# Stick-breaking attention summed by parts, with one sigmoid and the scan read from SBUF, in a hybrid SSM and attention block

## The chip, the cores and the metric

The kernel runs on one core of one Trainium2 chip. The core has five engines with queues of their own: TensorE (PE in the profile, with its weight loads apart as PEld), VectorE (DVE), ScalarE (ACT), GpSimd (POOL) and SyncE (SP), which here only issues DMAs. Instructions of one queue start in order; between queues they wait for semaphores. The metric is the device time of one execution in microseconds, as the median of several runs. Before the change it is 1559.6 us (three runs, 1559.3 to 1562.25).

## The reference, cut to what matters

One layer over 2048 tokens of width 1024. The input is normalised and projected; one half of the channels goes through a diagonal state-space model (SSM), the other half through stick-breaking attention with 8 heads of 64. Both are gated, projected out, added to the residual, and a gated embedding is added. The change touches the attention alone, and in it what follows the scores:

```python
z = jnp.einsum('bhqd,bhkd->bhqk', qb, kb) * scale
strict = s_pos < t_pos
log_stay = jnp.where(strict, jax.nn.log_sigmoid(-z), 0.0)
later = lax.cumsum(log_stay, axis=3, reverse=True) - log_stay
weights = jnp.where(strict, jnp.exp(jax.nn.log_sigmoid(z) + later), 0.0)
outs.append(jnp.einsum('bhqk,bhkd->bhqd', weights, vb))
```

For a query t and a key s before it, the weight is sigmoid(z[t, s]) times the product of sigmoid(−z[t, r]) over all r with s < r < t. Call P[s] the product over all r from s up to t − 1. Then the weight is P[s+1] − P[s], because 1 − sigmoid(−z) is sigmoid(z).

## The kernel before, in words

**Stages.** The SSM inputs are projected first, then comes the SSM with the gate's projections, then the attention, and at last the output projection and the embedding. The attention runs in 40 steps (`for t in range(steps)`). Four passes of two heads each (`hp`) start 8 steps apart, so that up to two passes are active in a step. In step t a pass computes the attention of query block i = t − 8 hp (`attn_block`, 128 queries), and then the projections of block i + 2 (`attn_proj`). In the last eight steps (from `glu_at` on) the SSM's output stage (`glu_unit`) and sums of weight blocks (`cross_sums`) are mixed in.

**Projections (`attn_proj`).** The normalised tokens `xt` come by a DMA on SP. PE multiplies them by one weight tile for q, k, v and the gate, in two halves of the contraction side by side, each into a PSUM bank of its own (`pq`, line 732). ACT copies the first bank to `part` (739, or 735 with a scale for the first two blocks), DVE adds the second: 384 columns to `qn` (740), 128 columns straight to the tile of v (741) that the attention multiplies later. The normalisation of q and k needs one power on POOL (501).

**Attention (`attn_block`).** Keys are taken in chunks of up to 512, from the newest back. Per chunk and for both heads:

1. PE writes the scores into a PSUM bank per head, `ps_z` (797). Up to step 31 three banks take turns (z0, z1, tr), in the last eight steps two (z0, z1).
2. ACT writes sigmoid(−z) to the SBUF tile `px` (802) and, after a border column was set by POOL (memset, 804) or copied by DVE from the chunk before (806), sigmoid(z) to the tile `be` (807).
3. In the newest chunk POOL masks the diagonal block of both tiles (811).
4. DVE turns `px` into running products from the right, in place (813). The scan is given the score bank as its second input; its second operation is a bypass, so that the values are not used.
5. POOL multiplies `be` by `px` shifted by one column (815). These are the weights.
6. PE transposes them into a pair of PSUM banks (`pw`, "ps_wt", line 520 of a helper), ACT copies them to `ws` (828), and PE multiplies them with v into `ps_o` (836). The same pair of banks also serves the transposes of q and k.

DVE multiplies the block's output by the gate into `yat`, and a DMA on SP stores it (840).

**Order.** All instructions get their place from a planner (`arrange`, `best_order`): it gives each an estimated duration, follows the dependences, keeps rows marked `abreast` together, and fixes the order on each queue, SP's DMAs among them. DVE operations with two SBUF inputs and POOL operations that read SBUF are planned one after the other. The buffers are counted by constants: `PXB` 4 tiles of `px`, `BEB` 6 of `be`. `BANKS` holds the PSUM banks of scores, projections and output, up to step 31 and after.

Of the kernel before, what the change touches and what calls it, by code (L numbers as in the profile page):

```python
# [18 lines left out]
P = 128  # L19
# [15 lines left out]
HD = 64  # L35
# [2 lines left out]
SKEW = 8  # L38
EPS = 1e-6
MAGIC = 12582912.0  # L40
XB, XTB, GTB, QSB, BEB, PXB, WSB, SWB, ROTB, STA, STB, STC, ALT, ALT0, ALT1, SSM_STEPS, SSM_DEPTH, PREP0, BEX, PXX, WSX, XTX, XT0 = 4, 2, 5, 5, 6, 4, 5, 2, 2, 3, 2, 3, "o", 0, 30, 10, 2, 0, 0, 0, 0, 0, 13
WE = 6
AHEAD = 4
BANKS = (("z0", "z1", "tr"), ("acc","ssm"), ("o",)), (("z0", "z1"), ("acc","tr"), ("o",))
WSV = lambda ch: 0
KV_SLOT = {(0, 0): 0, (0, 1): 1, (0, 2): 2, (1, 0): 3, (0, 3): 4, (1, 1): 5, (1, 2): 6, (2, 0): 7,
           (1, 3): 0, (2, 1): 1, (2, 2): 2, (3, 0): 4, (3, 1): 3, (2, 3): 5, (3, 2): 0, (3, 3): 1}
# [658 lines left out]
def attn_proj(e, pool, A, i, xt=None):  # L706

    nc = e.nc
    if xt is None:
        xt = e.buf("xt", [P, 2, NC8, P], XTB, XTX, F32R)  # L710
        e.xdma(xt.rearrange("p s c t -> p (s c t)").bitcast(F32), e.hn_d[i])
    both = pool.tile([P, 3 * HPP, HD], F32, tag="qn", name="qn", bufs=2)
    vb = A.v[i] = e.kv_tile(A.hp, i, "v", [P, HPP, HD])
    flat, vf = both.rearrange("p h d -> p (h d)"), vb.rearrange("p h d -> p (h d)")
    if len(e.q_banks) == 1:
        pq = e.bank("ps_qk", *e.q_banks)
        for c in range(NC8):
            mm3x(e, pq, (xt[:, 0, c], xt[:, 1, c]), (A.w[c][:, 0], A.w[c][:, 1]), c == 0, c == NC8 - 1)
        if i < 2:
            nc.scalar.activation(flat, pq[:, :384], AF.Copy, scale=e.rs[i])  # L720
            vs(nc, vf, pq[:, 384:], e.rs[i], ALU.mult)
        else:
            nc.scalar.activation(flat, pq[:, :384], AF.Copy)
            nc.vector.tensor_copy(vf, pq[:, 384:])
    else:
        pq = [e.bank(f"ps_q{h}", tag) for h, tag in enumerate(e.q_banks)]
        for c in range(NC8):
            with e.abreast():
                for s, (a, b) in enumerate(((0, 0), (0, 1), (1, 0))):
                    for h, o in enumerate(pq):  # L730
                        r = slice(64 * h, 64 * h + 64)
                        nc.tensor.matmul(o, xt[r, a, c], A.w[c][r, b], start=c + s == 0, stop=c == NC8 - 1 and s == 2)  # L732
        part = pool.tile([P, 512], F32, tag="part", name="part", bufs=1)
        if i < 2:
            nc.scalar.activation(part, pq[0], AF.Copy, scale=e.rs[i])
            stt(nc, flat, pq[1][:, :384], e.rs[i], part[:, :384], ALU.mult, ALU.add)
            stt(nc, vf, pq[1][:, 384:], e.rs[i], part[:, 384:], ALU.mult, ALU.add)
        else:
            nc.scalar.activation(part, pq[0], AF.Copy)
            vt(nc, flat, pq[1][:, :384], part[:, :384], ALU.add)  # L740
            vt(nc, vf, pq[1][:, 384:], part[:, 384:], ALU.add)
    raw, gate = both[:, :2 * HPP], flat[:, 256:]
    gn = pool.tile([P, P], F32, tag="gn", name="gn", bufs=1)
    nc.scalar.activation(gn, gate, AF.Sigmoid)
    vt(nc, gn, gate, gn, ALU.mult)
    sq = pool.tile([P, 2 * HPP, HD], F32, tag="sq", name="sq", bufs=1)
    nc.scalar.activation(sq, raw, AF.Square)
    ss = pool.tile([P, 2 * HPP], F32, tag="ssq", name="ssq", bufs=2)
    nc.vector.tensor_reduce(ss, sq, op=ALU.add, axis=AX.X)
    r = rms_rstd(e, pool, ss, 2 * HPP, HD, "qk")  # L750
    vt(nc, raw, raw, r.unsqueeze(2).to_broadcast([P, 2 * HPP, HD]), ALU.mult)
    qn = raw.rearrange("p (m h) d -> p m h d", m=2)
    if i % 4 == 0:
        A.k.append(e.kv_tile(A.hp, i, "k", [P, 2, 512]))
    q = pool.tile([P, 2, P], F32R, tag="q", name="q", bufs=QSB)
    views = [qn[:, m].rearrange("p h d -> p (h d)") for m in range(2)] + [gn]

    def whole(a):
        return a.rearrange("p (h t) -> p h t", h=2)

    if len(e.q_banks) == 1:
        ps = e.bank("ps_tq", "w0", "w1")
        for m, v in enumerate(views):
            nc.tensor.transpose(ps[:, m * P:(m + 1) * P], v, e.ident)
        tq, tk, tg = (whole(ps[:, P * m:P * m + P]) for m in range(3))
    else:
        ps = e.pair("ps_tq")
        with e.abreast():
            transposes(e, [ps[:, h] for h in range(2)], views)
        tq, tk, tg = (ps[:, :, 64 * m:64 * m + 64] for m in range(3))  # L770
    split(e, whole(q[:, 0]), whole(q[:, 1]), tq)
    k = A.k[-1][:, :, (i % 4) * P:(i % 4 + 1) * P]
    nc.scalar.activation(whole(k[:, 0]), tk, AF.Copy, scale=e.gqk)
    stt(nc, whole(k[:, 1]), tk, e.gqk, whole(k[:, 0]).bitcast(F32), ALU.mult, ALU.subtract)
    g = pool.tile([P, P], F32, tag="g", name="g", bufs=QSB)
    nc.scalar.activation(whole(g), tg, AF.Copy)
    A.q[i] = q, g


def attn_block(e, pool, A, i):  # L780

    nc = e.nc
    q, g = A.q.pop(i)
    half = [slice(HD * h, HD * (h + 1)) for h in range(HPP)]
    carry = [None] * HPP
    po = e.bank("ps_o", *e.o_banks)
    held = []
    for ch in range(i // 4, -1, -1):  # L790
        nb = min(4, i + 1 - 4 * ch)
        n = nb * P
        zs = [e.bank("ps_z", *e.z_banks) for _ in range(HPP)]
        with e.abreast():
            for s, (a, b) in enumerate(((0, 0), (0, 1), (1, 0))):
                for h, z in enumerate(zs):
                    nc.tensor.matmul(z[:, :n], q[half[h], a], A.k[ch][half[h], b, :n], start=s == 0, stop=s == 2)  # L797
        bes = []
        for h, z in enumerate(zs):
            be = e.buf("be", [P, 512], BEB, BEX)  # L800
            px = e.buf("px", [P, 513], PXB, PXX)
            nc.scalar.activation(px[:, :n], z[:, :n], AF.Sigmoid, scale=-(HD ** -0.5))  # L802
            if carry[h] is None:
                nc.gpsimd.memset(px[:, n:n + 1], 1.0)
            else:
                nc.vector.tensor_copy(px[:, n:n + 1], carry[h])
            nc.scalar.activation(be[:, :n], z[:, :n], AF.Sigmoid, scale=HD ** -0.5)  # L807
            if ch == i // 4:
                for a, fill in ((px, 1.0), (be, 0.0)):
                    d = a[:, n - P:n]  # L810
                    nc.gpsimd.affine_select(d, d, pattern=[[-1, P]], compare_op=ALU.is_gt, fill=fill, base=0, channel_multiplier=1)  # L811
            rv = px[:, :n][:, ::-1]
            nc.vector.tensor_tensor_scan(rv, rv, z[:, :n][:, ::-1], initial=1.0 if carry[h] is None else carry[h], op0=ALU.mult, op1=ALU.bypass)  # L813
            carry[h] = px[:, 0:1]
            nc.gpsimd.tensor_tensor(be[:, :n], be[:, :n], px[:, 1:n + 1], op=ALU.mult)  # L815
            bes.append(be)
        w = e.buf("ws", [P, HPP, 4, P], WSB, WSX)
        pw = e.pair("ps_wt")
        with e.abreast():
            transposes(e, [pw[:, h] for h in range(2)], [be[:, b * P:(b + 1) * P] for be in bes for b in range(nb)])  # L820
        for h in range(2):
            ps = pw[:, h, :64 * HPP * nb].rearrange("p (k t) -> p k t", t=64)
            dst = w[:, :, :nb, 64 * h:64 * h + 64]
            ps = ps.rearrange("p (h b) t -> p h b t", h=HPP)
            if h and WSV(ch):
                nc.vector.tensor_copy(dst, ps)
            else:
                nc.scalar.activation(dst, ps, AF.Copy)  # L828
        held.append((ch, nb, w))
        if len(held) == HOLD or ch == 0:  # L830
            with e.abreast():
                for c, n, w in held:
                    for b in range(n - 1, -1, -1):
                        sb = 4 * c + b
                        for h in range(HPP):
                            nc.tensor.matmul(po[half[h], :P], A.v[sb][:, h], w[:, h, b], start=sb == i, stop=sb == 0)  # L836
            held = []
    y = pool.tile([P, P], F32, tag="yat", name="yat", bufs=2)
    vt(nc, y, po[:, :P], g, ALU.mult)
    nc.sync.dma_start(e.ya_d[i][A.hp], y)  # L840


def attn_pass(e, hp):
    A = Env()
    A.hp, A.k, A.v, A.q, A.w = hp, [], {}, {}, []
    return A


# [178 lines left out]
def hybrid_block_kernel(ctx: ExitStack, tc: tile.TileContext, x, xt, small, p, w_in, ssm_w_glu, w_out, w_ple_gate,  # L1027
# [34 lines left out]
    make_identity(nc, e.ident)  # L1062
    e.mhalf = const("mhalf", [P, 2 * HPP])
    nc.vector.memset(e.mhalf, -0.5)
    e.rs = [const(f"rs{i}", [P, 1]) for i in range(2)]

    def part(name):
# [517 lines left out]
```

## Time and profile before

| | before |
|---|---|
| median of three runs | 1559.6 us |
| profiled execution | 1561.9 us |
| its span | 1560.2 us |
| PE, PEld busy | 1480.4, 1257.4 us |
| DVE, ACT, POOL busy | 1073.6, 938.7, 819.2 us |
| attention stage, 326.8 to 1166.8 us: span, PE busy | 840.0, 799.2 us |

How to read the rows: a group's row has line, engine, operation, output<-inputs, shapes and count; then busy us and the mean in ns of one; then the idle time of that engine just before, and what ended it. A row of a window has its length, then the busy time of each engine with its count, and at the end the clock that PE was granted (1.00 is full), the busy share of the DMA engines and GB/s. A row "A <- B: us, times, longest" is time in which A stood idle until B was done. "issue" is time in which an engine waited for nothing that the profile shows.

### The profile page before, as it was taken

To read this page: it belongs to the slowest core of one execution; us is meant where nothing else is said; L and a number is where in the kernel's file an instruction comes from. 1 tells how busy PE (TensorE), PEld (TensorE's weight loads), DVE (VectorE), ACT (ScalarE), POOL (GpSimd) and SP (SyncE) were. 2 spreads that over 40 slices of the span, in tenths; PEclk is the share of its full clock that TensorE was granted. 3 is DMA by queue.
4 is the path that set the end of the run, shared out by engine and by line. 5 is a ranking of instruction groups with operands and counts; after the bars stand their busy time and mean duration, and the time that the engine had idled before them with its cause. 6 is when DMAs were issued, how large, how long until landed. Compare 5 with 4: busy or idle time off the path is not lost.

```text
span 1560.2 us, 34921 instructions
## 1 busy us (share of the span) xinstructions
PE 1480.4 (95%) x13116; PEld 1257.4 (81%) x13116; DVE 1073.6 (69%) x2052; ACT 938.7 (60%) x2076; POOL 819.2 (53%) x1038
## 2 busy tenths in 40 slices
PE   5999999999999999998999988999998999999998
PEld 5999999978888788887887876777776888777776
DVE  8944868867667876778867776666869556754444
ACT  5654445557577877677777777766765435633432
POOL 3241433445455665565656688765565654433433
PEclk8999999999999989999999988999999999999999
DMA  8777735565332412234323466763448645612211
GB/s 294 272 250 222 237 119 188 165 198 163 116 116 99 150 67 98 105 116 128 99 94 112 138 213 180 220 184 93 112 136 257 199 161 183 200 63 94 89 62 61
DMA packets 168969, 236.21 MB, mean 151 GB/s; under 512 B 63664, under 2 KB 110816, under 8 KB 157408
## 3 DMA queue, kind: packets, MB, share of 16 engines
q1 hardware_dynamic: 166416, 225.38, 44.7%
q0 software_dynamic: 2384, 8.59, 2.0%
q8 instruction: 104, 1.70, 0.4%
q14 instruction: 65, 0.53, 0.1%
HBM read 169.03 MB, written 64.90 MB: 150 GB/s over the span
## 4 chain that ended last, share of the span: by engine, by line
PE 74%; DVE 9%; ACT 5%; issue 4%; DMA 4%; POOL 3%; POOLq 0%; SPq 0%; ACTq 0%; DVEq 0%
PE ps_q L732 19%; PE ps_o L836 6%; PE ps_z L797 5%; PE ps_wt L520 4%; PE ps_g L701 3%; PE ps_g L703 3%; PE ps_g L702 3%; PE ps_h L702 3%; PE ps_h L703 3%; PE ps_h L701 3%; DVE px L813 2%; PE ps_sg L535 2%; PE ps_sg L536 2%; PE ps_sg L537 2%; DMA wst<-in_ssm_w_glu_dram 2%
## 5 line engine op out<-in xcount | busy, mean ns | idle before, releaser
L815 POOL TENSOR_TENSOR be<-be,px 128x512 f32<-128x512 f32 (+3 forms) x320 | 317.6, 998 | 224.3 <-DVE px L813 177.1
L813 DVE TENSOR_TENSOR_SCAN px<-px,ps_z 128x512 f32<-128x512 f32 (+3 forms) x320 | 340.2, 1086 | 108.6 <-ACT be L807 81.8
L732 PE MATMUL ps_q<-w_w,xt 64*128 64x512 f32 x2880 | 400.9, 404 | 6.6 <-DVE v L65 3.6
L732 PEld LDWEIGHTS ps_q<-w_w,xt 64*128 64x128 f32 x2880 | 294.5, 187 | 43.8 <-PE ps_z L797 7.2
L828 ACT ACTIVATE ws<-ps_wt 128x512 f32<-128x512 f32 (+3 forms) x320 | 165.0, 547 | 76.2 <-PE ps_wt L520 75.9
L802 ACT ACTIVATE px<-ps_z 128x512 f32<-128x512 f32 (+3 forms) x320 | 162.4, 538 | 67.6 <-PE ps_z L797 48.7
L807 ACT ACTIVATE be<-ps_z 128x512 f32<-128x512 f32 (+3 forms) x320 | 168.7, 554 | 1.3 <-PE ps_wt L520 1.2
L797 PE MATMUL ps_z<-k,q 64*128 64x512 f32 (+3 forms) x960 | 146.3, 385 | 15.9 <-DVE px L813 12.4
L836 PE MATMUL ps_o<-ws,v 128*64 128x128 f32 x2176 | 139.8, 281 | 0.9 <-ACT ws L828 0.9
L836 PEld LDWEIGHTS ps_o<-ws,v 128*64 128x64 f32 x2176 | 121.0, 140 | 19.1 <-issue 15.5
L520 PEld LDWEIGHTS ps_wt<-ident,be 64*128 64x128 f32 x2176 | 101.1, 142 | 36.6 <-issue 15.3
L797 PEld LDWEIGHTS ps_z<-k,q 64*128 64x128 f32 x960 | 94.9, 189 | 35.0 <-DVE px L813 18.2
L520 PE MATMUL ps_wt<-ident,be 64*128 64x64 f32 x2176 | 108.5, 229 | 13.4 <-POOL be L815 4.8
L1008 POOL TENSOR_TENSOR sg<-sg,h 128x512 f32<-128x512 f32 x32 | 44.9, 1414 | 114.6 <-DVE sg L65 114.6
L501 POOL TENSOR_TENSOR rs_qk<-rs_qk,mhalf 128x4 f32<-128x4 f32 x64 | 66.6, 1040 | 39.7 <-DVE rs_qk L72 38.8
L535 PE MATMUL ps_u<-xt,w_w 128*128 128x256 f32 x256 | 74.8, 294 | 8.1 <-ACT w_w L485 7.0
L65 DVE TENSOR_TENSOR yr<-sx,yr 128x512 fp32r<-128x512 f32 x64 | 53.6, 858 | 34.6 <-ACT yr L507 33.7
L537 PE MATMUL ps_u<-xt,w_w 128*128 128x256 f32 x256 | 74.3, 296 | 3.0 <-DVE w_w L76 3.0
L536 PE MATMUL ps_u<-xt,w_w 128*128 128x256 f32 x256 | 74.8, 293 | 0.7 <-DVE xt L65 0.7
L507 ACT ACTIVATE yr<-sx 128x512 fp32r<-128x512 f32 x64 | 39.3, 629 | 50.8 <-POOL sx L894 20.2
L811 POOL TENSOR_SCALAR_AFFINE_SELECT px<-px 128x128 f32<-128x128 f32 x128 | 41.2, 332 | 50.4 <-ACT px L802 49.1
L1002 ACT ACTIVATE sg<-sg,rs 128x512 f32<-128x512 f32 x24 | 17.4, 724 | 73.6 <-DVE sg L65 73.6
(418 smaller groups left out, 3674.5 us busy)
## 6 DMA issues: line engine op xcount, KB each, us to landing
xt<-hn SPq DMA_DIRECT2D x60, 1024.0 KB, 4.9
hn<-xt SPq DMA_DIRECT2D x16, 1024.0 KB, 5.5
h<-h SPq DMA_DIRECT2D x64, 256.0 KB, 3.6
wst<-in_w_in_dram SPq DMA_DIRECT2D x48, 256.0 KB, 3.3
xg<-hn SPq DMA_DIRECT2D x12, 1024.0 KB, 6.7
out_dram<-sg SPq DMA_DIRECT2D x32, 256.0 KB, 2.5
x<-in_x_dram SPq DMA_DIRECT2D x14, 512.0 KB, 5.3
h<-in_x_dram SPq DMA_DIRECT2D x28, 256.0 KB, 4.7
```

The lines of the kernel that those rows point to most:

```text
L520: e.nc.tensor.transpose(ps[h][:, 64 * k:64 * k + 64], v[r], e.ident[r, r])
L535: mm(out, wh, xh, start=first, stop=False)
L536: mm(out, wh, xl, start=False, stop=False)
L537: mm(out, wl, xh, start=False, stop=last)
L732: nc.tensor.matmul(o, xt[r, a, c], A.w[c][r, b], start=c + s == 0, stop=c == NC8 - 1 and s == 2)
L797: nc.tensor.matmul(z[:, :n], q[half[h], a], A.k[ch][half[h], b, :n], start=s == 0, stop=s == 2)
L802: nc.scalar.activation(px[:, :n], z[:, :n], AF.Sigmoid, scale=-(HD ** -0.5))
L807: nc.scalar.activation(be[:, :n], z[:, :n], AF.Sigmoid, scale=HD ** -0.5)
L813: nc.vector.tensor_tensor_scan(rv, rv, z[:, :n][:, ::-1], initial=1.0 if carry[h] is None else carry[h], op0=ALU.mult, op1=ALU.bypass)
L815: nc.gpsimd.tensor_tensor(be[:, :n], be[:, :n], px[:, 1:n + 1], op=ALU.mult)
L828: nc.scalar.activation(dst, ps, AF.Copy)
L836: nc.tensor.matmul(po[half[h], :P], A.v[sb][:, h], w[:, h, b], start=sb == i, stop=sb == 0)
```

## The change

With P[s] as above and Q[s] = 1 − P[s], the output of a query is the sum over s of (P[s+1] − P[s]) v[s], and summed by parts this is the sum over s of Q[s] (v[s] − v[s−1]), with v[−1] = 0. So the new kernel

- drops the second sigmoid, the tile `be`, the mask on it, the border column and the product on POOL; the scan's result `px` is transposed itself;
- forms 1 − P while ACT copies the transposed tile to `ws`: Identity with scale −1 and a per-partition bias tile of ones, in place of Copy;
- keeps differences of v in place of v: the projection writes `vr`, a DMA on SP writes it shifted by one row into the tile `vb`, a second one brings the last row of the block before (for the first block a POOL memset), and POOL subtracts;
- gives the scan `px` in SBUF as its second input in place of the score bank, so that nothing but the sigmoid reads a score bank;
- up to step 31 takes two score banks in place of three, and lets the projections' two halves take turns over three banks in place of two;
- has 8 tiles of `px` with 512 columns in place of 4 with 513 and 6 of `be`.

```diff
-XB, XTB, GTB, QSB, BEB, PXB, ... = 4, 2, 5, 5, 6, 4, ...
+XB, XTB, GTB, QSB, PXB, ... = 4, 2, 5, 5, 8, ...
-BANKS = (("z0", "z1", "tr"), ("acc","ssm"), ("o",)), (("z0", "z1"), ("acc","tr"), ("o",))
+BANKS = (("z0", "z1"), ("acc", "ssm", "tr"), ("o",)), (("z0", "z1"), ("acc", "tr"), ("o",))
...
+    vr = pool.tile([P, P], F32, tag=f"vr{A.hp % 2}", name="vr", bufs=2)
-    flat, vf = both.rearrange("p h d -> p (h d)"), vb.rearrange("p h d -> p (h d)")
+    flat, vf, vb = both.rearrange("p h d -> p (h d)"), vr, vb.rearrange("p h d -> p (h d)")
...
-        pq = [e.bank(f"ps_q{h}", tag) for h, tag in enumerate(e.q_banks)]
+        pq = [e.bank("ps_q", *e.q_banks) for h in range(2)]
...
+    nc.sync.dma_start(vb[1:], vr[:P - 1])
+    if A.last is None:
+        nc.gpsimd.memset(vb[:1], 0.0)
+    else:
+        nc.sync.dma_start(vb[:1], A.last[P - 1:])
+    A.last = vr
+    nc.gpsimd.tensor_tensor(vb, vr, vb, op=ALU.subtract)
...
-            be = e.buf("be", [P, 512], BEB, BEX)
-            px = e.buf("px", [P, 513], PXB, PXX)
+            px = e.buf("px", [P, 512], PXB, PXX)
             nc.scalar.activation(px[:, :n], z[:, :n], AF.Sigmoid, scale=-(HD ** -0.5))
-            if carry[h] is None:
-                nc.gpsimd.memset(px[:, n:n + 1], 1.0)
-            else:
-                nc.vector.tensor_copy(px[:, n:n + 1], carry[h])
-            nc.scalar.activation(be[:, :n], z[:, :n], AF.Sigmoid, scale=HD ** -0.5)
             if ch == i // 4:
-                for a, fill in ((px, 1.0), (be, 0.0)):
-                    d = a[:, n - P:n]
-                    nc.gpsimd.affine_select(d, d, pattern=[[-1, P]], compare_op=ALU.is_gt, fill=fill, base=0, channel_multiplier=1)
+                d = px[:, n - P:n]
+                nc.gpsimd.affine_select(d, d, pattern=[[-1, P]], compare_op=ALU.is_gt, fill=1.0, base=0, channel_multiplier=1)
             rv = px[:, :n][:, ::-1]
-            nc.vector.tensor_tensor_scan(rv, rv, z[:, :n][:, ::-1], initial=1.0 if carry[h] is None else carry[h], op0=ALU.mult, op1=ALU.bypass)
+            nc.vector.tensor_tensor_scan(rv, rv, rv, initial=1.0 if carry[h] is None else carry[h], op0=ALU.mult, op1=ALU.bypass)
             carry[h] = px[:, 0:1]
-            nc.gpsimd.tensor_tensor(be[:, :n], be[:, :n], px[:, 1:n + 1], op=ALU.mult)
...
-                nc.scalar.activation(dst, ps, AF.Copy)
+                nc.scalar.activation(dst, ps, AF.Identity, bias=e.one, scale=-1.0)
...
+    e.one = const("one", [P, 1])
+    nc.vector.memset(e.one, 1.0)
```

More of the change, by code (lines that the diff above doesn't have):

```diff
@@ L40 @@
 MAGIC = 12582912.0
-XB, XTB, GTB, QSB, BEB, PXB, WSB, SWB, ROTB, STA, STB, STC, ALT, ALT0, ALT1, SSM_STEPS, SSM_DEPTH, PREP0, BEX, PXX, WSX, XTX, XT0 = 4, 2, 5, 5, 6, 4, 5, 2, 2, 3, 2, 3, "o", 0, 30, 10, 2, 0, 0, 0, 0, 0, 13
+XB, XTB, GTB, QSB, PXB, WSB, SWB, ROTB, STA, STB, STC, ALT, ALT0, ALT1, SSM_STEPS, SSM_DEPTH, PREP0, PXX, WSX, XTX, XT0 = 4, 2, 5, 5, 8, 5, 2, 2, 3, 2, 3, "o", 0, 30, 10, 2, 0, 0, 0, 0, 13
 WE = 6
 AHEAD = 4
-BANKS = (("z0", "z1", "tr"), ("acc","ssm"), ("o",)), (("z0", "z1"), ("acc","tr"), ("o",))
+BANKS = (("z0", "z1"), ("acc", "ssm", "tr"), ("o",)), (("z0", "z1"), ("acc", "tr"), ("o",))
 WSV = lambda ch: 0
@@ L797, in attn_block @@
                     nc.tensor.matmul(z[:, :n], q[half[h], a], A.k[ch][half[h], b, :n], start=s == 0, stop=s == 2)
-        bes = []
+        pxs = []
         for h, z in enumerate(zs):
-            be = e.buf("be", [P, 512], BEB, BEX)
-            px = e.buf("px", [P, 513], PXB, PXX)
+            px = e.buf("px", [P, 512], PXB, PXX)
             nc.scalar.activation(px[:, :n], z[:, :n], AF.Sigmoid, scale=-(HD ** -0.5))
-            if carry[h] is None:
-                nc.gpsimd.memset(px[:, n:n + 1], 1.0)
-            else:
-                nc.vector.tensor_copy(px[:, n:n + 1], carry[h])
-            nc.scalar.activation(be[:, :n], z[:, :n], AF.Sigmoid, scale=HD ** -0.5)
             if ch == i // 4:
-                for a, fill in ((px, 1.0), (be, 0.0)):
-                    d = a[:, n - P:n]
-                    nc.gpsimd.affine_select(d, d, pattern=[[-1, P]], compare_op=ALU.is_gt, fill=fill, base=0, channel_multiplier=1)
+                d = px[:, n - P:n]
+                nc.gpsimd.affine_select(d, d, pattern=[[-1, P]], compare_op=ALU.is_gt, fill=1.0, base=0, channel_multiplier=1)
             rv = px[:, :n][:, ::-1]
-            nc.vector.tensor_tensor_scan(rv, rv, z[:, :n][:, ::-1], initial=1.0 if carry[h] is None else carry[h], op0=ALU.mult, op1=ALU.bypass)
+            nc.vector.tensor_tensor_scan(rv, rv, rv, initial=1.0 if carry[h] is None else carry[h], op0=ALU.mult, op1=ALU.bypass)
             carry[h] = px[:, 0:1]
-            nc.gpsimd.tensor_tensor(be[:, :n], be[:, :n], px[:, 1:n + 1], op=ALU.mult)
-            bes.append(be)
+            pxs.append(px)
         w = e.buf("ws", [P, HPP, 4, P], WSB, WSX)
@@ L819, in attn_block @@
         with e.abreast():
-            transposes(e, [pw[:, h] for h in range(2)], [be[:, b * P:(b + 1) * P] for be in bes for b in range(nb)])
+            transposes(e, [pw[:, h] for h in range(2)], [px[:, b * P:(b + 1) * P] for px in pxs for b in range(nb)])
         for h in range(2):
@@ L825, in attn_block @@
             if h and WSV(ch):
-                nc.vector.tensor_copy(dst, ps)
+                vs(nc, dst, ps, -1.0, ALU.mult, 1.0, ALU.add)
             else:
-                nc.scalar.activation(dst, ps, AF.Copy)
+                nc.scalar.activation(dst, ps, AF.Identity, bias=e.one, scale=-1.0)
         held.append((ch, nb, w))
@@ L844, in attn_pass @@
     A = Env()
-    A.hp, A.k, A.v, A.q, A.w = hp, [], {}, {}, []
+    A.hp, A.k, A.v, A.q, A.w, A.last = hp, [], {}, {}, [], None
     return A
```

## The prediction

> **What bounds the kernel now.** I read the page's busy shares first, then the attention stage by windows, then who holds TensorE (PE) there, then the rows of each operation that the change touches.
>
> ```profile
> PE 1480.4 (95%) x13116; PEld 1257.4 (81%) x13116; DVE 1073.6 (69%) x2052; ACT 938.7 (60%) x2076; POOL 819.2 (53%) x1038
> PE 74%; DVE 9%; ACT 5%; issue 4%; DMA 4%; POOL 3%; POOLq 0%; SPq 0%; ACTq 0%; DVEq 0%
> ```
> PE is busy 95% of the span and holds 74% of the chain that ended last: taking work from another engine pays only where PE waited for it. The first score product starts at 326.8 us and the last attention output is written at about 1166.8. Those 840 us, in three windows with their sum:
>
> ```profile
> 326.80:900.00 573.20, 547.79 (x6539) 468.79 (x6541) 425.46 (x852) 416.05 (x1035) 341.08 (x593) 0.99 0.36 120
> 900.00:1000.00 100.00, 88.52 (x958) 71.31 (x957) 65.95 (x112) 72.41 (x157) 81.88 (x107) 0.90 0.70 210
> 1000.00:1166.80 166.80, 162.89 (x1454) 128.03 (x1450) 115.83 (x170) 112.96 (x225) 99.82 (x116) 1.00 0.48 133
> sum 840.00, PE 799.20 PEld 668.12 DVE 607.24 ACT 601.42 POOL 522.79; mean PE 266.40 PEld 222.71 DVE 202.41 ACT 200.47 POOL 174.26
> ```
> Columns: busy time of PE, weight loads, DVE, ACT, POOL, then granted clock, DMA share, GB/s. PE stands idle 840 − 799.2 = 40.8 us, most densely (11.5 of 100) in the second window, where the clock is also lowest. PE's own waits in this stage (total us, times, longest):
>
> ```profile
> PE ps_z L797 <- DVE px L813: 12.4, 11, 2.4
> PE ps_wt L520 <- POOL be L815: 4.8, 4, 1.8
> PE ps_wt L520 <- issue: 4.2, 8, 1.6
> PE ps_q L732 <- DVE v L65: 3.6, 7, 0.8
> PE ps_wt L520 <- ACT ws L828: 3.2, 2, 2.0
> PE ps_q L732 <- DVE px L806: 1.7, 2, 0.9
> PE ps_q L732 <- DVE v L76: 1.2, 1, 1.2
> PE ps_wt L520 <- POOL px L811: 0.4, 1, 0.4
> ```
> The largest is a score product waiting for the scan, which reads the score bank itself. One such wait in the timeline:
>
> ```profile
> 543.80 0.60 ACT L802 ACTIVATE px<-ps_z 128x512 f32<-128x512 f32 x1 [0.36 <-PE ps_z L797]
> 544.92 1.28 DVE L813 TENSOR_TENSOR_SCAN px<-px,ps_z 128x512 f32<-128x512 f32 x1
> 546.25 1.64 PE L797 MATMUL ps_z<-k,q 64*128 64x512 f32 x5 [1.58 <-DVE px L813]
> ```
> The sigmoid ends at 544.40, the scan at 546.20, and only then does the next score product go on.
>
> **Lost clock.** After such stalls the granted clock is low:
>
> ```profile
> 540.00:560.00 20.00, 17.40 (x186) 15.33 (x186) 16.16 (x32) 15.45 (x36) 11.30 (x16) 0.83 0.27 85
> 570.00:580.00 10.00, 8.42 (x84) 6.54 (x82) 9.13 (x20) 7.74 (x18) 6.14 (x6) 0.83 0.32 112
> 920.00:940.00 20.00, 15.84 (x182) 13.41 (x184) 12.91 (x24) 13.97 (x31) 17.22 (x24) 0.74 0.53 183
> 950.00:970.00 20.00, 15.50 (x176) 13.36 (x177) 12.55 (x21) 13.20 (x29) 15.83 (x27) 0.74 0.47 132
> ```
> Missing clock times busy PE: 0.17 × 17.4 + 0.17 × 8.4 + 0.26 × 15.8 + 0.26 × 15.5 = 12.5 us.
>
> **The change part by part.** The rows that price it, from the page and from the groups kept apart by shape:
>
> ```profile
> L815 POOL TENSOR_TENSOR be<-be,px 128x512 f32<-128x512 f32 (+3 forms) x320 | 317.6, 998 | 224.3 <-DVE px L813 177.1
> L813 DVE TENSOR_TENSOR_SCAN px<-px,ps_z 128x512 f32<-128x512 f32 (+3 forms) x320 | 340.2, 1086 | 108.6 <-ACT be L807 81.8
> L807 ACT ACTIVATE be<-ps_z 128x512 f32<-128x512 f32 (+3 forms) x320 | 168.7, 554 | 1.3 <-PE ps_wt L520 1.2
> L815 POOL TENSOR_TENSOR be<-be,px 128x128 f32<-128x128 f32 x32 | 12.9, 422 | 4.3 <-DVE px L806 3.2 <-DVE rs_qk L72 0.6 <-DVE px L813 0.4
> L811 POOL TENSOR_SCALAR_AFFINE_SELECT be<-be 128x128 f32<-128x128 f32 x128 | 40.1, 320 | 10.8 <-ACT be L807 9.8
> L806 DVE COPY px<-px 128x1 f32<-128x1 f32 x192 | 23.8, 141 | 0.1
> L804 POOL MEMSET px<- 128x1 f32 x128 | 11.3, 101 | 6.0 <-ACT gsq L462 6.0
> ```
>
> *Second sigmoid, product, second mask, border column.* ACT loses 168.7 us; POOL 317.6 + 40.1 + 11.3 = 369 us; DVE 23.8 us. None of it is PE time, so it is worth only the PE waits above. PE's waits on POOL's product (4.8), on the mask (0.4) and on the border copy (1.7) have no instruction left to wait for: 6.9 us. The product was the last step before the transposes; the scan is late next, about 1.0 us sooner (998 ns a product). The transposes read px in place of be, as many and as large, and one more constant is set at the start: nothing.
>
> *Scan from SBUF, two score banks.* A bank is now freed by its one sigmoid instead of sigmoid, sigmoid, scan. In the example it comes free at 544.40 instead of 546.20, 1.8 us sooner. Up to step 31 a third bank now goes: both heads of the next chunk need the two banks just used, where before one of the two was the spare, so the second head's sigmoid (0.6 us) is waited for as well. Net 1.2 us sooner. In the last eight steps the kernel before has two banks already, and the whole 1.8 us is gained. The waits are 12.4 / 11 = 1.1 us each, so I take all 12.4. Bounds: 12.4 gained, or 12.4 kept, if ACT, in order, serves evictions between the two sigmoids.
>
> *Three banks for the projections.* Two of three rotate; the next projection needs the spare and the bank that ACT drains, not the one that DVE drains. PE's 3.6 + 1.2 us on DVE's v go: 4.8 us.
>
> Direct sum: 12.4 + 6.9 + 4.8 = 24.1 us, 59% of the 40.8 idle. The clock follows the stalls, so 59% of 12.5: 7.4 us more (bounds 0 and 12.5).
>
> *Eviction with scale and bias.* The nearest rows are the projection's eviction with and without a per-partition operand:
>
> ```profile
> L739 ACT ACTIVATE part<-ps_q x54: 591/601/666, 339.0 to 1100.7; 128x512 f32<-128x512 f32 x54
> L735 ACT ACTIVATE part<-ps_q,rs x6: 687/688/736, 385.2 to 769.3; 128x512 f32<-128x512 f32 x6
> ```
> 87 ns more on 320 evictions: 28 us on ACT, which still ends 141 us lighter. They hold the transposes' bank pair longer, and PE waits for that pair 3.2 us now. Upper bound 28 us, lower 0; the pair is in use about half of the time, so I take 0.5.
>
> *Differences of v.* Each of 64 projections gets a shift by DMA (127 rows of 512 B), a second DMA of one row (60 times) or a memset (4), and a POOL subtraction of 128x128. The last costs 422 ns by the row above: 25 us on POOL in this stage, covered by the 369 removed. The DMAs are priced by the block output, one row per kind of issue:
>
> ```profile
> ya<-yat SPq DMA_DIRECT2D x63, 64.0 KB, 2.0
> 624.58 0.32 SPq L840 DMA_DIRECT2D ya<-yat  x1
> SPq L840 <- DVE yat L65: 125.3, 30, 11.3
> ```
> 2.0 us to land, 0.32 us to issue: 40 us of SP's time. They wait for DVE's v and stand ahead of later xt loads on SP; behind the subtraction, on POOL's queue, stand the masks and the power. SP already waits 125.3 us for yat in the same way. A projection made at the end of one step is first used two steps on, so a whole step lies between; 40 steps in 840 us are 21 us each, ten landings. The work that hides the round trip is that step. I take 0; bounds 0 and 2.0 us for each of 60, 120 us.
>
> *The scan's second input.* It reads px twice from SBUF instead of px and a bank (in the SSM stage there are scans of that kind already). The groups by shape give both kinds:
>
> ```profile
> L813 DVE TENSOR_TENSOR_SCAN px<-px,ps_z 128x512 f32<-128x512 f32 x224 | 277.7, 1262 | 85.1 <-ACT be L807 70.3 <-POOL px L811 7.6 <-POOL px L804 4.3
> L409 DVE TENSOR_TENSOR_SCAN swp<-decf,rot 128x512 f32<-128x512 f32 x8 | 9.8, 1221 | 0.2
> ```
> 41 ns less on 512 columns, 11 us over all. Against it, a scan with two SBUF inputs met a POOL operation once in this trace:
>
> ```profile
> 198.41 1.23 DVE L438 TENSOR_TENSOR_SCAN rot<-decf,rot 128x512 f32<-128x512 f32 x1
> 198.54 1.93 POOL L501 TENSOR_TENSOR rs_qk<-rs_qk,mhalf 128x4 f32<-128x4 f32 x1 [6.35 <-DVE rs_qk L72]
> 204.76 1.02 POOL L501 TENSOR_TENSOR rs_qk<-rs_qk,mhalf 128x4 f32<-128x4 f32 x1 [2.02 <-DVE rs_qk L72]
> ```
> The power took 0.91 us longer beside the scan. I expect the reverse too: a scan behind a POOL operation waits. POOL keeps 523 − 369 + 25 = 179 us, 21% of the stage, in operations of 0.3 to 1.4 us: about 0.1 us a scan, 32 us, against 24 + 11 saved. DVE stays near 607 of 840 and costs PE nothing; at worst 1.02 us a scan, 326 us. The Trainium skill ("SBUF — State Buffer", section "Who interferes with whom") states that a DVE instruction with two SBUF inputs contends with a GpSimd instruction that reads SBUF, and one with at most one SBUF input does not. By that rule all 320 scans join the contention that they are free of now, which speaks against the change; the 1.93 beside 1.02 agrees with it. By the rows' overlap the sum stays 1529; by the rule taken to its end, every scan behind a whole power, DVE would hold 572 + 326 = 898 us, 58 beyond the stage, and the time would be 1618.
>
> Sum against the profiled execution (1561.9, span 1560.2): −24.1 − 7.4 + 0.5 = −31.0, so 1530.9. The median of the runs, 1559.6, is 2.3 lower: 1529.
>
> **Rivals.**
> *PE at full density.* If all 40.8 us of idle and 12.5 of clock go, 1559.6 − 53 = 1506. For it: slack grows on every chain. Against: 4.2 + 3.2 us of waits are untouched, and the order is fixed beforehand.
> *The gain is hidden.* PE's waits move to the transposes' pair (evictions 28 us longer in total) and to ACT's queue between two sigmoids: 24.1 + 7.4 − 28 leaves 3.5, so 1556, with 1552 to 1562 around it. For it: ACT is in order, and PE already waits 3.2 us for ws. Against: ACT loses 141 us.
> *Slower by the shared read path.* DVE would be 607 − 35 + 320 w, w the wait of a scan for POOL. It overtakes PE's 799 from w = 0.71 us; at 0.75 it is 812, and at PE's present density of 95% the stage takes 855, 15 more: 1575. For it: the stretched power. Against: POOL is left at 21%, so w near 0.1. This is where the skill's rule above would be felt.
> *Slower by the round trip.* A subtraction that waits for its DMA holds POOL's masks, the masks the scans, these PE. It decides from 0.52 us of PE for each of 60 (31 us); at 1.0 us, half a landing, 1589. For it: DMA share 0.70 in the second window. Against: two steps of slack.
>
> **How the numbers follow.** 0.2% is 3.1 us, about what a measurement of this kernel can tell from no change. Forecast 0.62 (its own range 1515 to 1546); full density 0.10; hidden 0.15, of which 0.10 still faster and 0.05 the same; read path 0.08; round trip 0.05. Faster 0.82, same 0.05, slower 0.13. The range reaches from full density, 1507, to the top of the hidden case, 1558, which leaves out the two slower cases and a little of the first.
>
> **What would show it.** Right: no PE wait of ps_z on the scan, and ps_z held by the sigmoid only; PE idle in the stage under 20 us with its windows at clock 1.00; POOL under 200 us there; evictions near 0.69 us; scans near 1.22. Wrong: scans well over 1.3 us mean, or PE waiting for ws, for the differences of v, or for xt; a projection that starts late behind the new DMAs on SP.

## The result, and the profile after

The changed kernel takes 1543.3 us (median of four runs, 1538.9 to 1544.2) against 1560.9 us before: a ratio of 0.988 with a 95% interval of 0.9856 to 0.9905. It is faster by 17.6 us, where 31 were forecast. The profiled execution took 1544.2 us with a span of 1542.4; both kernels are compared by their profiled executions below.

The page of the changed kernel, its busy shares, the chain by engine, and the groups that were priced (the scan a second time for its 512 columns alone):

```profile
PE 1476.5 (96%) x13116; PEld 1250.9 (81%) x13116; DVE 1030.0 (67%) x1861; ACT 835.0 (54%) x1756; POOL 552.0 (36%) x530
PE 74%; DVE 7%; DMA 5%; issue 5%; POOL 3%; ACT 3%; SPq 2%; POOLq 0%; ACTq 0%; DVEq 0%
L814 DVE TENSOR_TENSOR_SCAN px<-px 128x512 f32<-128x512 f32 (+3 forms) x320 | 362.1, 1152 | 47.0 <-ACT px L809 32.9
L814 DVE TENSOR_TENSOR_SCAN px<-px 128x512 f32<-128x512 f32 x224 | 292.7, 1329 | 36.3 <-ACT px L809 32.9 <-POOL px L812 2.4
L828 ACT ACTIVATE ws<-ps_wt,one 128x512 f32<-128x512 f32 (+3 forms) x320 | 188.2, 624 | 89.4 <-PE ps_wt L520 89.0
L501 POOL TENSOR_TENSOR rs_qk<-rs_qk,mhalf 128x4 f32<-128x4 f32 x64 | 81.0, 1266 | 178.5 <-DVE rs_qk L72 178.5
L812 POOL TENSOR_SCALAR_AFFINE_SELECT px<-px 128x128 f32<-128x128 f32 x128 | 62.6, 498 | 174.1 <-ACT px L809 167.4
L749 POOL TENSOR_TENSOR v<-vr,v 128x128 f32<-128x128 f32 x64 | 41.2, 644 | 182.9 <-DMA v<-vr 179.0
```
ACT lost 104 us and POOL 267 us over the span, and PE's share rose by one point. SP's queue and the DMAs came up in the chain that ended last: before, DMA had 4% of it and SPq 0%; now 5% and 2%.

The attention stage, from the first score product to the last gated output, in the windows used before:

```profile
328.20:900.00 571.80, 559.85 (x6754) 475.31 (x6756) 401.45 (x737) 356.45 (x827) 151.49 (x217) 0.98 0.39 132
900.00:1000.00 100.00, 89.56 (x906) 69.77 (x904) 67.17 (x87) 59.57 (x116) 58.94 (x48) 0.93 0.70 211
1000.00:1149.00 149.00, 145.68 (x1293) 113.61 (x1292) 97.73 (x121) 83.05 (x154) 44.28 (x41) 0.99 0.48 134
sum 820.80, PE 795.10 PEld 658.68 DVE 566.35 ACT 499.06 POOL 254.71; mean PE 265.03 PEld 219.56 DVE 188.78 ACT 166.35 POOL 84.90
```
The stage takes 820.8 us (840.3 before, measured to the same event). PE's idle time fell from 40.8 to 25.7 us, and its busy time for the same matmuls from 799.5 to 795.1. The other stages together take 721.6 us, 719.9 before. The granted clock is 0.98, 0.93 and 0.99 in the three windows, against 0.99, 0.90 and 1.00.

What PE waited for in this stage of the changed kernel (us, times, longest):

```profile
PE ps_z L805 <- ACT px L809: 8.4, 12, 3.3
PE ps_wt L520 <- ACT ws L828: 4.8, 4, 3.4
PE ps_g L535 <- ACT zr L507: 4.0, 2, 3.3
PE ps_h L701 <- ACT yr L507: 1.9, 1, 1.9
PE ps_q L733 <- ACT part L740: 0.9, 3, 0.3
```
No score product waits for the scan any more, PE waits for nothing of POOL, and the projections wait 0.9 us. But scores now wait 8.4 us for the sigmoid. The longest of these waits, 3.3 us, stands in the timeline; ACT had stood for a weight block's DMA twice just before:

```profile
709.75 0.63 ACT L507 ACTIVATE w_w<-wst 128x512 fp32r<-128x512 f32 x1 [1.69 <-DMA wst<-in_ssm_w_glu_dram]
712.36 0.63 ACT L507 ACTIVATE w_w<-wst 128x512 fp32r<-128x512 f32 x1 [1.98 <-DMA wst<-in_ssm_w_glu_dram]
713.15 1.07 ACT L809 ACTIVATE px<-ps_z 128x512 f32<-128x512 f32 x2
713.79 2.13 PE L805 MATMUL ps_z<-k,q 64*128 64x512 f32 x6 [3.31 <-ACT px L809]
```

The instructions around the tile `vr` in the changed kernel (ns, minimum, median, maximum), the shift's issue, the one row's issue and the subtraction:

```profile
L743 SPq DMA_DIRECT2D v<-vr x64: 622/634/842, 197.7 to 1087.0; - x64
L747 SPq DMA_DIRECT2D v<-vr x60: 548/1946/7957, 206.1 to 1087.7; - x60
L749 POOL TENSOR_TENSOR v<-vr,v x64: 453/462/1382, 203.3 to 1092.5; 128x128 f32<-128x128 f32 x64
```
From the shift's issue to the subtraction 5.6 us pass at the first block (197.7 to 203.3) and 5.5 at the last. The row of 512 B holds SP for 1.95 us in the median and up to 8.0. In the chain of this stage SP's issue of it has 2.1% (17 us) and the landing of these DMAs 1.7% (14 us). Three of its longest pieces, and what stood behind one of them:

```profile
723.47 4.69 SPq L747
728.26 7.71 DMA wst<-in_ssm_w_glu_dram
...
882.29 7.96 SPq L747
...
985.36 4.82 SPq L747
```
A weight block was issued only when SP came free at 728.16, and landed 7.7 us later. A landing stands in the same chain with POOL's queue behind it: the subtraction, two operations on another tile, the power, and then DVE and PE (the other pieces between these are left out):

```profile
933.52 5.21 DMA v<-vr
938.91 0.10 POOL v L749
942.43 0.98 POOL rs_qk L501
943.43 1.51 DVE qn L65
945.08 0.40 PE ps_tq L520 x6
```

### The profile page after: what moved, and what is told of

Same layout as the page of the kernel before. It is cut to its first block, busy times and chain, and to the rows that moved or that the text cites. A ratio compares the mean times of both kernels' runs of the same rounds, so it can differ in the third digit from the quotient of the medians.

```text
span 1542.4 us, 33653 instructions
## 1 busy us (share of the span) xinstructions
PE 1476.5 (96%) x13116; PEld 1250.9 (81%) x13116; DVE 1030.0 (67%) x1861; ACT 835.0 (54%) x1756; POOL 552.0 (36%) x530
## 4 chain that ended last, share of the span: by engine, by line
PE 74%; DVE 7%; DMA 5%; issue 5%; POOL 3%; ACT 3%; SPq 2%; POOLq 0%; ACTq 0%; DVEq 0%
PE ps_q L733 20%; PE ps_o L836 6%; PE ps_z L805 6%; PE ps_wt L520 4%; PE ps_h L701 3%; PE ps_g L701 3%; PE ps_h L702 3%; PE ps_h L703 3%; PE ps_g L703 3%; PE ps_g L702 3%; PE ps_u L537 1%; PE ps_u L536 1%; PE ps_u L535 1%; SPq L747 1%; PE ps_sg L535 1%
## 5 line engine op out<-in xcount | busy, mean ns | idle before, releaser
L814 DVE TENSOR_TENSOR_SCAN px<-px 128x512 f32<-128x512 f32 (+3 forms) x320 | 362.1, 1152 | 47.0 <-ACT px L809 32.9
L733 PEld LDWEIGHTS ps_q<-w_w,xt 64*128 64x128 f32 x2880 | 286.2, 188 | 43.4 <-issue 4.5
L828 ACT ACTIVATE ws<-ps_wt,one 128x512 f32<-128x512 f32 (+3 forms) x320 | 188.2, 624 | 89.4 <-PE ps_wt L520 89.0
L501 POOL TENSOR_TENSOR rs_qk<-rs_qk,mhalf 128x4 f32<-128x4 f32 x64 | 81.0, 1266 | 178.5 <-DVE rs_qk L72 178.5
L812 POOL TENSOR_SCALAR_AFFINE_SELECT px<-px 128x128 f32<-128x128 f32 x128 | 62.6, 498 | 174.1 <-ACT px L809 167.4
L520 PEld LDWEIGHTS ps_wt<-ident,px 64*128 64x128 f32 x2176 | 95.6, 141 | 31.6 <-ACT ws L828 13.0
L520 PE MATMUL ps_wt<-ident,px 64*128 64x64 f32 x2176 | 104.1, 228 | 5.0 <-ACT ws L828 4.8
L749 POOL TENSOR_TENSOR v<-vr,v 128x128 f32<-128x128 f32 x64 | 41.2, 644 | 182.9 <-DMA v<-vr 179.0
L65 DVE TENSOR_TENSOR qn<-ps_q,part 128x384 f32<-128x384 f32 x54 | 29.7, 551 | 59.6 <-ACT part L740 46.1
L65 DVE TENSOR_TENSOR yr<-yq,yr 128x512 fp32r<-128x512 f32 x48 | 50.6, 1056 | 14.1 <-ACT yr L507 13.9
```

Of the source, the lines that this page charges most:

```text
L65: nc.vector.tensor_tensor(out, a, b, op=op)
L520: e.nc.tensor.transpose(ps[h][:, 64 * k:64 * k + 64], v[r], e.ident[r, r])
L814: nc.vector.tensor_tensor_scan(rv, rv, rv, initial=1.0 if carry[h] is None else carry[h], op0=ALU.mult, op1=ALU.bypass)
L828: nc.scalar.activation(dst, ps, AF.Identity, bias=e.one, scale=-1.0)
```

## The experiments

The theory after the result: the direct waits went as forecast, and what is missing was taken by the round trip of the differences, by SP's issue of the one row above all. The rivals: the new waits for ACT and the slower scans; or only the order that the planner drew.

**The row issued from POOL's queue.**

```diff
-        nc.sync.dma_start(vb[:1], A.last[P - 1:])
+        nc.gpsimd.dma_start(vb[:1], A.last[P - 1:])
```


> The changed kernel, with the one-row DMA of the differences issued from POOL's queue in place of SP's. Theory: what is missing of the forecast gain was lost because SP stands 1.9 us (median, up to 8.0) in issuing that DMA and the weight loads behind it come late; then SP's queue is free, PE's idle in the attention stage falls from 26 us by about half, and the time falls by about 10 us, to 1533. Rival: SP's issue time is hidden and the missing gain went into ACT's order and the scan's longer duration; then the time stays within 3 us of 1543.

Measured: 1537.2 us, ratio to the kernel before 0.9862 (0.9833 to 0.989); stage 808.2 us. The row's issue takes 0.56 us there. It lies between the two expectations, and its interval overlaps that of the change.

**No differences at all.**

```diff
-    nc.sync.dma_start(vb[1:], vr[:P - 1])
...
-    nc.gpsimd.tensor_tensor(vb, vr, vb, op=ALU.subtract)
```
(the row's DMA and `vr` go too)

> The changed kernel without the differences: v goes straight to its tile, no shift DMA, no row DMA, no subtraction (the output is then the sum of Q times v, left without the differencing). It prices the whole round trip. Theory (SP and POOL held by it): 12 to 15 us less than 1543, about 1530. Rival (round trip hidden): within 3 us of 1543.

Measured: 1527.4 us, 0.9793 (0.9767 to 0.9819); stage 804.0 us, PE idle 18.3. That is a little past the theory's number, and close to the forecast of 1529, for which the round trip was counted as nothing. The stage is 16.8 us shorter than in the changed kernel: 7.4 of idle PE and 9.4 of PE's busy time for the matmuls.

**The scan given the score bank again.**

```diff
-            nc.vector.tensor_tensor_scan(rv, rv, rv, ...
+            nc.vector.tensor_tensor_scan(rv, rv, z[:, :n][:, ::-1], ...
```


> The changed kernel with the scan's second input given back to the score bank: the bank is held until the scan has ended, and the scan no longer reads SBUF twice. Theory: the early release of the banks carries most of the gain; 16 us or more are lost (with only two banks, perhaps 25), 1559 to 1570. Rival: reading SBUF twice costs more than the bank gives (the scans of 512 columns took 1329 ns in place of 1262): the time falls, 1540 or less.

Measured: 1554.5 us, 0.9973 (0.9956 to 0.9989); stage 835.7 us, PE idle 35.8. It lost 11 us, between the two expectations; the experiments below with another order show that a time this close proves nothing by itself, so the waits have to decide. The waits of PE and the groups of this kernel:

```profile
PE ps_z L805 <- DVE px L814: 11.7, 12, 1.9
```
```profile
L814 DVE TENSOR_TENSOR_SCAN px<-px,ps_z 128x512 f32<-128x512 f32 (+3 forms) x320 | 335.6, 1084 | 166.4 <-POOL px L812 86.3 <-ACT px L809 79.3
L501 POOL TENSOR_TENSOR rs_qk<-rs_qk,mhalf 128x4 f32<-128x4 f32 x64 | 66.8, 1044 | 245.8 <-DVE rs_qk L72 245.8
L812 POOL TENSOR_SCALAR_AFFINE_SELECT px<-px 128x128 f32<-128x128 f32 x128 | 40.5, 326 | 146.9 <-ACT px L809 146.0
L749 POOL TENSOR_TENSOR v<-vr,v 128x128 f32<-128x128 f32 x64 | 31.7, 495 | 185.2 <-DMA v<-vr 185.1
```
The wait for the bank is back at 11.7 us, close to the 12.4 before: the bank is what the scan's second input decides. The same rows show what the second SBUF input goes with in the changed kernel: there the scans took 1152 ns against 1084 here, the masks 498 against 326, the power 1266 against 1044, the subtraction 644 against 495.

**The banks of the kernel before.**

```diff
-BANKS = (("z0", "z1"), ("acc", "ssm", "tr"), ("o",)), ...
+BANKS = (("z0", "z1", "tr"), ("acc", "ssm"), ("o",)), ...
```


> The changed kernel with the banks of the kernel before: three for scores, two for projections up to step 31. Theory: PE waits again for DVE's v at the start of a projection, 4.8 us as before, and with the clock 6 us: 1549. Rival: a third score bank is worth more now that scores wait for ACT (8.4 us): 1538.

Measured: 1538.0 us, 0.986 (0.9823 to 0.9898); stage 815.1 us. The rival's number, but scores still wait 5.7 us for the sigmoid; the experiment with 9 tiles below shows that 5 us prove nothing here. The theory's wait did not come back: with two banks PE waited 0.3 us for v at the start of projections, where the kernel before had 4.8.

**Only the row left out.**

```diff
-    if A.last is None:
-        nc.gpsimd.memset(vb[:1], 0.0)
-    else:
-        nc.sync.dma_start(vb[:1], A.last[P - 1:])
+    nc.gpsimd.memset(vb[:1], 0.0)
```


> The changed kernel without the one-row DMA: the first row of each block's differences is set to zero by POOL before the subtraction (what a block's first row takes from the block before is left out). The shift of 127 rows stays on SP. With the row on POOL's queue the time was 1537, without any shift 1527. Theory (SP's long issue of the one row is the larger part): 1535 or less. Rival (the round trip itself, POOL waiting 3 us for each landing, is the larger part): 1537 to 1543.

Measured: 1530.5 us, 0.981 (0.9794 to 0.9826); stage 809.2 us. The theory's number: 13 of the 16 us come without the one row, though POOL still waits as long for the shift (179 us in all before the subtraction, as in the changed kernel). But the long issue did not go with the row. The block output's store, 0.32 us elsewhere, now takes it where it stands right behind the shift:

```profile
376.83 0.62 SPq L743 DMA_DIRECT2D v<-vr  x1
377.50 2.61 SPq L837 DMA_DIRECT2D ya<-yat  x1
406.85 0.32 SPq L837 DMA_DIRECT2D ya<-yat  x1
```
The five stores issued within 0.1 us of a shift's issue took 2.3 to 3.7 us.

**Both DMAs from POOL's queue.** As above, and the shift on `nc.gpsimd` too.

> The changed kernel with both DMAs of the differences issued from POOL's queue, SP's queue as in the kernel before. Theory (what costs is SP's time): 1530 to 1534, near the 1527 without any shift. Rival (what costs is POOL's queue standing in front of its landing): not better than the 1537 with only the row on POOL, as POOL now also waits for DVE's v with masks behind it.

Measured: 1527.5 us, 0.9781 (0.9758 to 0.9803), with the whole computation. Its stage, and the instructions around `vr`:

```profile
332.40:1128.00 795.60, 784.12 (x8944) 645.24 (x8945) 570.62 (x943) 498.37 (x1095) 323.49 (x421) 0.98 0.46 146
```
```profile
L743 POOL DMA_DIRECT2D v<-vr x64: 546/594/634, 198.8 to 1068.3; - x64
L749 POOL TENSOR_TENSOR v<-vr,v x64: 446/492/1487, 200.9 to 1071.4; 128x128 f32<-128x128 f32 x64
L747 POOL DMA_DIRECT2D v<-vr x60: 503/512/590, 208.6 to 1068.9; - x60
```
PE idles 11.5 us of 795.6, the least of all. A row is issued in 0.51 us here, and the subtraction follows the shift's issue by 2.1 us at the first block and 3.1 at the last, in place of 5.6 and 5.5. The time is below the theory's. The rival did not come as it was told: POOL's queue stands 194 us in the stage in front of the shift, most of it for DVE's v, and the time falls all the same. That SP's time is what was saved is not shown by this time alone, since the kernel with the row first, below, keeps both DMAs on SP and takes 1525.

**The scan alone, in the kernel before.**

```diff
-            nc.vector.tensor_tensor_scan(rv, rv, z[:, :n][:, ::-1], ...
+            nc.vector.tensor_tensor_scan(rv, rv, rv, ...
```


> The kernel before with one edit: the scan's second input is px in SBUF, so that a score bank is held by the two sigmoids only. Theory (the bank's release carries 12.4 us and its clock): 1548, PE's 12.4 us on the scan gone. Rival (reading SBUF twice beside POOL's 320 products, which also read SBUF, holds both up): no gain or slower, 1560 to 1580, scans well over 1.3 us.

Measured: 1618.0 us, 1.0369 (1.0351 to 1.0387): the rival, and past its number. The stage, and the groups by shape:

```profile
324.60:1210.30 885.70, 818.54 (x8936) 667.72 (x8936) 679.17 (x1134) 599.98 (x1415) 658.90 (x811) 0.96 0.39 124
```
```profile
L813 DVE TENSOR_TENSOR_SCAN px<-px 128x512 f32<-128x512 f32 x224 | 346.6, 1557 | 13.9 <-ACT px L802 11.8 <-POOL px L811 1.3
L815 POOL TENSOR_TENSOR be<-be,px 128x512 f32<-128x512 f32 x224 | 312.2, 1405 | 151.1 <-DVE px L813 71.3 <-DVE px L806 38.9 <-ACT be L807 7.6
```
Scans went from 1262 to 1557 ns and products from 1140 to 1405: each takes longer beside the other. The wait of scores for the scan is gone here too (10.0 us of waiting for the second sigmoid took its place), and PE idles 67 us. The contention of two SBUF inputs with POOL's reads, as the Trainium skill states it ("SBUF — State Buffer", section "Who interferes with whom"), fits what this kernel shows, and the trace agrees: 1557 ns in place of 1262, 1405 in place of 1140. How much of the 57 us is these longer instructions and how much the planner's order is not separated: the planner, too, places scans with two SBUF inputs and POOL's reads one after the other.

**Row on POOL and banks of before together.**

> The changed kernel with both edits that gained alone: the one-row DMA on POOL's queue (1537) and the banks of the kernel before (1538). If they remove different waits, 1532; if each was only another order drawn by the planner, 1537 to 1543.

Measured: 1535.9 us, 0.9849 (0.9821 to 0.9876); stage 813.8 us. The gains do not add.

**The product alone, in the kernel before.**

```diff
-            nc.gpsimd.tensor_tensor(be[:, :n], be[:, :n], px[:, 1:n + 1], op=ALU.mult)
```


> The kernel before with one edit: POOL's product of the second sigmoid and the running product is left out (the transposes then take the bare sigmoid, so the running product does not enter the output). Banks and scan as before. Theory (the product costs PE only the waits seen): 4.8 + 0.4 us and a share of the clock, 1553. Rival (POOL's queue with the product holds up more than PE's own waits show): 1545 or less.

Measured: 1547.3 us, 0.9929 (0.9907 to 0.9952); stage 828.7 us, PE idle 33.8. PE's wait for POOL is gone, 11.5 us of waiting for the scan stay. The 11.6 us gained are between the two expectations.

**Both DMAs on POOL, with the banks of before.**

> The kernel with both DMAs on POOL's queue (1527) and in addition the banks of the kernel before. If the earlier gain of these banks (1538 against 1543) was a wait of its own, 1522; if it was another order drawn by the planner, 1525 to 1532.

Measured: 1532.3 us, 0.983 (0.9813 to 0.9846); stage 800.4 us. The highest value that was expected of another order: the banks have no gain of their own that these runs show.

**Nine tiles of px.** `PXB` 9 in place of 8.

> The changed kernel with 9 tiles of px in place of 8, an edit that should remove no wait: PE does not wait for px's buffers. It shows how far another order drawn by the planner moves the time by itself. Expected: within 4 us of 1543. If it moves by 10 us or more, differences of that size between the other runs prove nothing.

Measured: 1533.9 us, 0.9838 (0.9816 to 0.986); stage 809.6 us. 9 us less for an edit that removes no wait: the order that the planner draws moves the time that far, and differences of that size between the other runs prove nothing by the time alone.

**The row ahead of the shift in the code.**

```diff
-    nc.sync.dma_start(vb[1:], vr[:P - 1])
     if A.last is None:
         nc.gpsimd.memset(vb[:1], 0.0)
     else:
         nc.sync.dma_start(vb[:1], A.last[P - 1:])
+    nc.sync.dma_start(vb[1:], vr[:P - 1])
```


> The changed kernel with the two DMAs of the differences in the other order in the code: the one row of the block before (which is ready a projection earlier) ahead of the shift, both on SP. Theory 1 (SP's 1.9 us come from issuing right behind the 127-row shift): the row issues in about 0.6 us, and the time falls towards the 1530 without it. Theory 2 (a row of 512 B, cut into 32 packets, is slow to issue by itself): it still takes about 1.9 us wherever it stands, and the time stays within 3 us of 1543.

Measured: 1525.3 us, 0.9785 (0.9769 to 0.9801), the lowest median of all, with the whole computation; by its ratio it is level with both DMAs on POOL (0.9781). SP's queue in this kernel (line 747 is the shift, 746 the row):

```profile
409.30 0.65 SPq L747 DMA_DIRECT2D v<-vr  x1
410.00 2.56 SPq L746 DMA_DIRECT2D v<-vr  x1
...
894.32 2.36 SPq L840 DMA_DIRECT2D ya<-yat  x1
896.73 0.57 SPq L746 DMA_DIRECT2D v<-vr  x1
```
```profile
L746 SPq DMA_DIRECT2D v<-vr x60: 540/2040/7018, 197.4 to 1046.3; - x60
324.80:1134.30 809.50, 787.76 (x8944) 656.46 (x8945) 565.18 (x943) 498.96 (x1096) 258.55 (x302) 0.99 0.46 144
```
The planner put 56 of the 60 rows behind the shift again, and these issue as slowly as before. The four that stand behind another DMA took 0.56 to 0.65 us. With the stores of the kernel without the row this speaks for the first theory of the issue: what stands right behind the shift is slow, a row or not. The time fell without the issues getting shorter. What changed is the chain of the stage: it holds 1.4 us of the row's issue and no landing of the differences, against 17 and 14 us in the changed kernel, 10 and 8 with the banks of before, and 5 and 0 with nine tiles. By these pieces the four kernels stand in the same sequence as by their time, which speaks for them as the cause, but another order changes everything else on the chain as well.

**Taken together.** The stage's length in the profiled execution and the median time, by where the differences' DMAs are issued, all with one sigmoid and the scan from SBUF:

| differences | stage, us | time, us |
|---|---|---|
| both DMAs on SP: the change; banks of before; row first; 9 tiles | 820.8; 815.1; 809.5; 809.6 | 1543.3; 1538.0; 1525.3; 1533.9 |
| shift on SP, no row | 809.2 | 1530.5 |
| shift on SP, row on POOL; with banks of before | 808.2; 813.8 | 1537.2; 1535.9 |
| both on POOL; with banks of before | 795.6; 800.4 | 1527.5; 1532.3 |
| none | 804.0 | 1527.4 |

Order alone moves the first group by 11 us of stage and 18 us of time: the changed kernel drew the slowest of four. By the stage, the kernels that issue nothing for the differences on SP lie below all others. By the whole time they do not: the other stages take from 716.5 us (row first) to 731.7 (both on POOL), where the stage also starts up to 8 us later, and 1525.3 us with both DMAs on SP is as good as any. So among the experiments only the 57 us of the scan in the kernel before stand clear of the order; for the rest the waits and the chains have to speak. The change itself is faster in each of these four orders, but other orders of the kernel before were not run.

## Why the prediction was right or wrong

Time and direction came out as forecast (1543 in the range of 1507 to 1558, faster), but the gain was 17.6 in place of 31, near the slow end of the forecast's own range of 1515 to 1546. In the profiled executions the span fell by 17.8 us: PE's idle time in the stage by 15.1 (23.6 taken: 24.1 − 0.5), PE's busy time there by 4.4 (7.4 taken), and the other stages took 1.7 more (0 taken). Of the signs named for being right, PE idle under 20 us, windows at clock 1.00, POOL under 200 us and scans near 1.22 us did not come (25.7; 0.93 to 0.99; 255; 1.33 for 512 columns). By the steps:

- *Second sigmoid, product, mask, border.* The 6.9 us went: no PE wait on POOL or the border copy is left.
- *Scan from SBUF, two score banks.* The wait on the scan went whole, as taken, and came back at 11.7 us when only the scan's input was given back. But 8.4 us of waiting for the sigmoid took its place, 3.3 of them where ACT stood on a late weight block. The lower bound named this: ACT is in order, though there it was copies of weights that stood in front and not evictions. Net 4.0 of 12.4.
- *Three banks for the projections.* 0.9 of 4.8 us are left, 3.9 gained. The third bank is not shown to be the reason: with two in its place PE waited 0.3 us for v (1.2 and 1.7 with the row or both DMAs on POOL).
- *Clock: a step that failed.* 7.4 us were taken because "The clock follows the stalls". The stalls fell and the clock did not rise: missing clock times busy PE, counted as in the prediction but over the whole stage in windows of 10 us, is 14.1 us before and 16.5 after. PE's busy time fell by 4.4 us all the same, for a reason that these rows do not show. Without the differences the same count is 10.2 us, and it is 10.2 with the row first.
- *Eviction.* 689 ns in the mean of the 512-column tiles (610 before), as forecast; PE's wait for ws rose by 1.6, 0.5 taken. ACT ended 104 us lighter, not 141.
- *The scan's second input.* The size was right: 1329 ns for 512 columns is the 1221 of the SSM's scan and the 0.1 us taken for POOL. POOL holds 255 us in the stage, not 179: its own masks, powers and subtractions take longer too, beside the scans. The trace before had three meetings of a scan of this kind with a POOL operation, not one, and neither of the two scans of 512 columns among them took more than 1.23 us. The slower rival did not come, since w stayed near 0.1; with the product still there, it did. That this took 1618 us, the number worked out for the rule taken to its end, is chance: DVE was busy 679 us of that stage, not 898.
- *Differences of v: the step that failed most plainly.* The round trip was taken as nothing, with 0.32 us of SP's time and 2.0 us to land for each DMA, by the block output, and a whole step as cover. The cover held for v itself: PE never waited for a difference. What was sized wrong is the DMA: 0.63 us to issue the shift, 1.95 for what stands right behind it, and 5.5 us from the shift's issue to the subtraction. 17 us of the chain are the row's issue, with a weight block late behind it, and 14 us are landings, with POOL's queue late behind them. With both DMAs off SP the kernel reaches 1527, without differences 1527, and the forecast was 1529. The last agreement is partly luck: without differences PE's idle time fell by 22.5 us (23.6 taken), but its busy time by 13.8 (7.4 taken), and the other stages took 1.9 more.

Of the two slower rivals the round trip was the one that took part of the gain: in part as it was told, a landing that holds POOL's queue and through it DVE and PE, and in part by holding SP, which it did not name. How much of the 16 us is the round trip and how much the order drawn is not settled: both kinds of edit reach 1525 to 1534.

## What to carry to other kernels

An edit that takes work from an engine off the chain is worth the waits of the bound engine and no more; read those, and then price what the edit adds to every queue, the DMA queue too, by a row of the same shape of DMA: a shift of 127 rows is no block of 128, and what stands behind it on the queue pays as well. A gain in clock is not to be taken in proportion to the stalls removed; here it did not come. Parts of a change can depend on each other: the scan from SBUF costs 57 us while POOL's product is there, and takes away 11.7 us of PE's waiting once it is gone. Where a planner orders the work, draw several orders of the same work before a difference of one per cent is put down to an edit.

## What the runs showed of the hardware that was not expected

- A DMA issued on SP right behind one of 127 rows of 512 B takes long to issue: a row of 512 B 1.95 us in the median (0.55 to 8.0), a store of 128 rows 2.3 to 3.7 us in place of 0.32. Of the eight rows that stand behind another DMA on SP, in three kernels, seven took 0.56 to 0.65 us and one 1.72; on POOL's queue a row takes 0.51 to 0.56. Why SP takes so long stays open.
- With the row left out the profile counts 1920 packets fewer for 60 rows, 32 for each.
- The 127-row shift moves slowly: with nothing else in flight, in the kernel without the row, the DMA engines are busy for 0.07 of the time at 22 GB/s, so that its 65 KB take about 3 us (an estimate from the row below).
- A scan of 512 columns with both inputs in SBUF took 1557 ns beside POOL's products, 1329 beside its smaller operations and 1221 in the SSM stage.
- The same work in another order took from 1525 to 1543 us.
- The granted clock does not simply follow PE's idle time: 25.7 us of idle with 16.5 us of missing clock in the changed kernel, 33.8 with 8.1 in the kernel before without the product.

```profile
406.00:406.50 0.50, 0.50 (x8) 0.41 (x8) 0.30 (x1) 0.38 (x3) 0.20 (x2) 1.00 0.07 22
```
